# Encoder trunk on one core: raw weight buffers of the output projection from five to three, and another transfer model in the list schedule

## The chip, the cores and the metric

The kernel runs on one core of one Trainium2 chip. The metric is the device time in microseconds of one execution; the median of several runs is compared. The program runs TensorE (matrix products), VectorE, ScalarE, GpSimd and SyncE side by side; each takes its instructions strictly in the order in which they stand in its own program, and they wait for each other by semaphores. In the profile they are called PE (its weight loads PEld), DVE, ACT, POOL and SP. SP does nothing here but issue loads; POOL issues transfers too, through a queue of its own.

## The reference

A bidirectional encoder trunk of two layers over 512 positions of 1024 channels, all in float32. Of each layer this matters here:

```
xn = rms_norm(x, ln1[l]);  z = xn @ w_in[l]
y_a = gated linear recurrence, y_b = spatial gating, y_c = windowed attention
merged = (gates[:, :, 0] * (y_a @ w_br[l, 0])
          + gates[:, :, 1] * (y_b @ w_br[l, 1])
          + gates[:, :, 2] * (y_c @ w_br[l, 2]))
x = x + merged @ w_out[l]
hn = rms_norm(x, ln2[l])
x = x + square(relu(hn @ w_up[l])) @ w_down[l]
```

## The kernel before

**Products.** Every large product is made of three float32r products: an operand is split into a high part and a rest, and high x high, rest x high and high x rest are added up in PSUM. For weights the split runs on two engines: ScalarE casts the raw weight tile to its high part (`wh`, L546), VectorE subtracts (`wl`, L547). A raw weight tile is 128 x 1024 float32, 512 KB, and comes by one load that SP issues. There are three pairs of `wh`/`wl` (WB = 3), two raw buffers `wr` for weights in general (WR = 2), nine `wq` buffers for weights that are loaded further ahead, and, in the output projection alone, a set of raw buffers `wz`, whose number is WZ (L469).

**Stage Y2.** Between the branches and the MLP stands, in each layer, a stage that the program calls Y2. Names that matter, in order:

- `yA`: the product of branch A with its projection, made in two halves of the columns. Each half uses two raw weight tiles of `wr`. Of the second half in layer 0 these are number 921 and number 924 (in layer 1 the numbers are 1664 higher; the two layers have the same order).
- `mC` (four tiles for each half): the gated sum of branches C and A; L1610 and L1611 on VectorE make it from `yA`.
- `turn_sum` (L1581): `mC` is transposed by TensorE into a PSUM bank (`mT`, L1586), the sum with branch B is loaded back from memory (`mB`, L1592, issued by POOL), and VectorE adds the two (L1595). For the first half, numbers 892, 896, 900 and 909, the transposes use the two banks of the group "c": the third and the fourth can only start when the first and the second addition have emptied these banks.
- `project_out` (L854): the output projection by a Strassen-like scheme with seven products for its first half, each with one raw tile `wz`, numbered by ORDER = 1, 2, 6, 7, 0, 5, 4, 3 (0 is the place where `turn_sum` of the second half stands); then four more `wz` tiles for the rest. The weights of products 6, 7, 5 and 4 are sums that were made ahead and lie in the memory `wsd`; the others come from `in_ws_dram`. The operands `sh` and `mg` are made from `mB` by VectorE and ScalarE.
- Two `wr` tiles, number 1076 and number 1081, are already weights of the MLP that follows.

**What sets the order.** The program is first recorded. For two long spans a list scheduler then orders the instructions of each engine and pins the order: from Y2 of layer 0 to the input products of layer 1, and from Y2 of layer 1 to the end. The class `Order` does it: `plan` (L185) goes forward in modelled time, takes for each engine among the instructions that are ready the one that can start first (in a tie the one with the earliest due time `dead`), and for SP does not issue a load more than LEAD = 20 us before it is due. Loads in flight are modelled by one number `serve`: the time at which a single shared pipe has moved all that was issued so far, at 344 bytes per ns, and the transfers follow each other in it in the order of issue, whichever engine issued them. The model's durations only choose the order; on the chip the semaphores decide when things run.

## Time and profile before

| | us |
|---|---|
| median of 3 runs | 1644.1 (1643.7 to 1644.46) |
| profiled execution | 1641.78 |
| its span | 1640.0 |
| TensorE busy in it | 1617.2 |
| VectorE busy | 1385.2 |
| ScalarE busy | 1113.2 |
| both load queues together, mean | 147 GB/s |

TensorE is busy nearly all the time, so time can only go where it waits or where its clock is low. A row of a timeline gives the start and the length of an instruction (or of several alike) in microseconds, the engine, the line, the operation, the tiles as output<-inputs, and in brackets how long the engine stood idle before it and what ended that. Matmuls that follow each other overlap in such rows; the distance of their starts is what one costs. Rows of the chain of work give start, length and name only.

### The profile page before, as it was taken

To read this page: it belongs to the slowest core of one execution; us is meant where nothing else is said; L and a number is where in the kernel's file an instruction comes from. 1 tells how busy PE (TensorE), PEld (TensorE's weight loads), DVE (VectorE), ACT (ScalarE), POOL (GpSimd) and SP (SyncE) were. 2 spreads that over 40 slices of the span, in tenths; PEclk is the share of its full clock that TensorE was granted. 3 is DMA by queue.
4 is the path that set the end of the run, shared out by engine and by line. 5 is a ranking of instruction groups with operands and counts; after the bars stand their busy time and mean duration, and the time that the engine had idled before them with its cause. 6 is when DMAs were issued, how large, how long until landed. Compare 5 with 4: busy or idle time off the path is not lost.

```text
span 1640.0 us, 26186 instructions
## 1 busy us (share of the span) xinstructions
PE 1617.2 (99%) x9689; PEld 1391.4 (85%) x9689; DVE 1385.2 (84%) x2261; ACT 1113.2 (68%) x1941; POOL 222.3 (14%) x303
## 2 busy tenths in 40 slices
PE   9999999999899999999999999999998999999997
PEld 7888888888788998989888888888887888989896
DVE  8798979677689988888999869886886799888888
ACT  7666567676267777777756555886862677777774
POOL 0011001110310111111110110011002101121210
PEclk9999999999999999999999999999999999999999
DMA  8343224732756575766243332256327565766651
GB/s 323 103 154 113 78 91 132 172 110 85 276 141 206 141 190 145 193 146 151 103 163 121 128 121 78 78 157 162 107 90 281 122 213 146 189 156 166 167 129 52
DMA packets 76335, 240.94 MB, mean 147 GB/s; under 512 B 9680, under 2 KB 9936, under 8 KB 76208
## 3 DMA queue, kind: packets, MB, share of 16 engines
q1 hardware_dynamic: 45216, 157.58, 28.8%
q0 software_dynamic: 30560, 81.15, 21.3%
q8 instruction: 76, 1.25, 0.3%
q10 hardware_dynamic: 432, 0.55, 0.1%
q14 instruction: 51, 0.42, 0.1%
HBM read 196.25 MB, written 28.31 MB: 137 GB/s over the span
## 4 chain that ended last, share of the span: by engine, by line
PE 82%; DVE 6%; issue 5%; DMA 3%; ACT 2%; POOL 1%; SPq 0%; POOLq 0%; DVEq 0%; ACTq 0%
PE us L943 5%; PE us L944 5%; PE us L945 5%; PE dA L782 3%; PE dA L783 3%; PE dA L784 3%; DVE wl L547 2%; DMA mB<-mgd 2%; PE f L553 2%; PE f L552 2%; PE f L551 2%; PE gA L784 2%; PE gA L782 2%; PE gA L783 2%; PE at L1049 2%
## 5 line engine op out<-in xcount | busy, mean ns | idle before, releaser
L547 DVE TENSOR_TENSOR wl<-wq,wh 128x1024 fp32r<-128x1024 f32 x238 | 290.8, 1224 | 42.8 <-ACT wh L546 42.4
L546 ACT CAST wh<-wq 128x1024 fp32r<-128x1024 f32 x238 | 249.6, 1050 | 98.9 <-PE us L944 15.1
L546 ACT CAST wh<-wr 128x1024 fp32r<-128x1024 f32 x140 | 146.6, 1047 | 121.2 <-DMA wr<-in_ws_dram 42.1
L547 DVE TENSOR_TENSOR wl<-wr,wh 128x1024 fp32r<-128x1024 f32 x140 | 171.1, 1222 | 47.6 <-ACT wh L546 47.2
L943 PE MATMUL us<-xs,wh 128*128 128x256 f32 x448 | 127.0, 283 | 0.0
L945 PE MATMUL us<-xs,wl 128*128 128x256 f32 x448 | 126.7, 283 | 0.0
L944 PE MATMUL us<-xs,wh 128*128 128x256 f32 x448 | 126.7, 283 | 0.0
L832 POOL DMA_DIRECT2D xr<-dx x84 | 72.9, 868 | 393.9 <-ACT dx L831 382.5
L783 PE MATMUL dA<-wh,sh 128*128 128x512 f32 x256 | 100.0, 391 | 0.0
L784 PE MATMUL dA<-wl,sh 128*128 128x512 f32 x256 | 99.8, 391 | 0.0
L782 PE MATMUL dA<-wh,sh 128*128 128x512 f32 x256 | 99.4, 392 | 0.0
L943 PE MATMUL us<-xh,wh 128*128 128x256 f32 x336 | 95.6, 284 | 0.0
L944 PE MATMUL us<-xl,wh 128*128 128x256 f32 x336 | 95.0, 283 | 0.0
L945 PE MATMUL us<-xh,wl 128*128 128x256 f32 x336 | 95.0, 283 | 0.0
L943 PEld LDWEIGHTS us<-xs,wh 128*128 128x128 f32 x448 | 85.7, 191 | 0.4
L944 PEld LDWEIGHTS us<-xs,wh 128*128 128x128 f32 x448 | 85.8, 192 | 0.0
L945 PEld LDWEIGHTS us<-xs,wl 128*128 128x128 f32 x448 | 85.8, 192 | 0.0
L1077 DVE TENSOR_TENSOR ex<-ex 128x512 f32<-128x512 f32 x112 | 75.0, 688 | 3.8 <-ACT kt L1068 3.6
L943 PEld LDWEIGHTS us<-xh,wh 128*128 128x128 f32 x336 | 64.3, 191 | 1.5
L944 PEld LDWEIGHTS us<-xl,wh 128*128 128x128 f32 x336 | 64.4, 192 | 0.8
L945 PEld LDWEIGHTS us<-xh,wl 128*128 128x128 f32 x336 | 64.4, 192 | 0.0
L1065 ACT ACTIVATE qt<-ex 128x512 f32<-128x512 f32 x56 | 37.9, 677 | 35.0 <-DVE ex L1077 33.2
(467 smaller groups left out, 4999.7 us busy)
## 6 DMA issues: line engine op xcount, KB each, us to landing
wq<-in_ws_dram SPq DMA_DIRECT2D x140, 512.0 KB, 4.6
wr<-in_ws_dram SPq DMA_DIRECT2D x126, 512.0 KB, 3.7
xr<-dx POOLq DMA_DIRECT2D x84, 256.0 KB, 4.0
wsd<-in_ws_dram POOLq DMA_DIRECT2D x22, 512.0 KB, 8.0
thd<-zt POOLq DMA_DIRECT2D x32, 256.0 KB, 2.4
gt<-thd POOLq DMA_DIRECT2D x32, 256.0 KB, 3.9
wq<-in_ws_dram POOLq DMA_DIRECT2D x16, 512.0 KB, 7.6
wz<-in_ws_dram SPq DMA_DIRECT2D x14, 512.0 KB, 4.5
```

The source lines that it names most:

```text
L546: nc.scalar.copy(hi, raw)
L547: nc.vector.tensor_tensor(lo, raw, hi.bitcast(F32), ALU.subtract)
L551: nc.tensor.matmul(pt, whi, xhi, start=first, stop=False)
L782: nc.tensor.matmul(pt, xh[:, t], hi[:, c], start=start and k == 0, stop=False, skip_group_check=True)
L783: nc.tensor.matmul(pt, xl[:, t], hi[:, c], start=False, stop=False, skip_group_check=True)
L784: return nc.tensor.matmul(pt, xh[:, t], lo[:, c], start=False, stop=k == 3, skip_group_check=True)
L832: nc.gpsimd.dma_start(xr[t][fl], z, accum_op=ALU.add)
L943: nc.tensor.matmul(pt, hi[:, c], xh, start=n in (1, 2, 7) and k == 0, stop=False, skip_group_check=True)
L944: nc.tensor.matmul(pt, hi[:, c], xl, start=False, stop=False, skip_group_check=True)
L945: nc.tensor.matmul(pt, lo[:, c], xh, start=False, stop=k == 3, skip_group_check=True)
L1065: nc.scalar.activation(qt.rearrange(shp, b=nb, h=2), e_q, AF.Exp)
L1077: nc.vector.tensor_tensor(o_ap, o_ap, ap_of(ex, i_, [[istep, 2]] + z), ALU.add)
```

## The change

Two things. WZ, the number of raw buffers of the output projection, goes from 5 to 3. And the list scheduler's model of transfers is another: instead of one pipe in order of issue, each issuing engine has its own queue of bytes in flight (`serve[e]`), the queues that have work share the rate evenly (`pass_time`), and a transfer lands when its own queue is through, while the other queue takes its share (`landed`). A new test `crowds` holds back a load when, with the loads that are due before it, it would delay one of these; if nothing else can run, the test is dropped for one step (`polite`).

```diff
-LEAD = 20000.0
+LEAD, SPARE = 20000.0, 0.0
...
-        start, line, late, serve = {}, {e: [] for e in ready}, head, 0.0
+        start, line, late, serve = {}, {e: [] for e in ready}, head, dict.fromkeys(ready, 0.0)
+        clock = [0.0]
+        loads = sorted((dead[n.at], n.at) for n in seg if n.eng == "SP" and n.bytes)
...
+        def pass_time(t):
+
+            left_ = t - clock[0]
+            clock[0] = max(t, clock[0])
+            while left_ > 1e-6 and any(v > 1e-6 for v in serve.values()):
+                on = [k for k, v in serve.items() if v > 1e-6]
+                d = min([left_ / len(on)] + [serve[k] for k in on])
+                for k in on:
+                    serve[k] -= d
+                left_ -= d * len(on)
+
+        def landed(e, came, work):
+            pass_time(came)
+            serve[e] += work
+            mine, other = serve[e], sum(v for k, v in serve.items() if k != e)
+            return max(came, clock[0]) + mine + min(mine, other)
+
+        def crowds(c, now):
+
+            own = 2.0 * ops[c].bytes / 360.0
+            t = now + 1550 + 2.0 * serve["SP"]
+            for d, x in loads:
+                if d >= dead[c]:
+                    return False
+                if x in start or any(self.slots[i][0] in [self.slots[j][0] for j in ops[c].first] for i in ops[x].first):
+                    continue
+                t += 2.0 * ops[x].bytes / 360.0
+                if 0.0 < t + own - (d + late + 2900 + ops[x].bytes / 344.0 - SPARE) < own:
+                    return True
+            return False
...
                     if e == "SP":
                         s = max(s, dead[c] + late - LEAD)
+                        if polite and crowds(c, s):
+                            continue
...
-                serve = max(serve, s + n.occ + (1000 if e == "Pool" else 1500) + (1700 if n.add else 0)) + n.bytes / (215.0 if n.add else 344.0)
-                end[c] = serve + 445
+                end[c] = landed(e, s + n.occ + (1000 if e == "Pool" else 1500) + (1700 if n.add else 0), n.bytes / (215.0 if n.add else 360.0)) + 445
...
-    BYDMA, EARLY, ORDER, WZ = (1, 6, 7, 5), (), (1, 2, 6, 7, 0, 5, 4, 3), 5
+    BYDMA, EARLY, ORDER, WZ = (1, 6, 7, 5), (), (1, 2, 6, 7, 0, 5, 4, 3), 3
```

No instruction is added or left out. The order on POOL stays as it was. On the other four engines it moves at a few places, alike in the two layers: at the head of Y2 and inside it, in the first quarter of the MLP, and in layer 0 a little at the passage to the next layer. The new lines push the later line numbers up: L862 becomes L900, L527 L565, L547 L585, L1595 L1633, L602 L640, L1610 L1648, L1611 L1649.

First, SP at the head of Y2 in layer 0, before. A row is one load, destination<-source; the first number of a name is the tile's number, the second one counts on.

```order
L862 DMA wz_938_4581<-in_ws_dram 128x1024
L862 DMA wz_945_4607<-in_ws_dram 128x1024
L862 DMA wz_948_4625<-wsd0_215 128x1024
L862 DMA wz_955_4651<-wsd0_215 128x1024
L862 DMA wz_976_4723<-wsd0_215 128x1024
L527 DMA wr_924_4524<-in_ws_dram 128x1024
L527 DMA wr_1076_5097<-in_ws_dram 128x1024
L527 DMA wr_1081_5131<-in_ws_dram 128x1024
L862 DMA wz_981_4747<-wsd0_215 128x1024
L862 DMA wz_984_4765<-in_ws_dram 128x1024
```

And the same ten loads of SP in the changed program:

```order
L900 DMA wz_938_4581<-in_ws_dram 128x1024
L900 DMA wz_945_4607<-in_ws_dram 128x1024
L565 DMA wr_924_4524<-in_ws_dram 128x1024
L900 DMA wz_948_4625<-wsd0_215 128x1024
L565 DMA wr_1076_5097<-in_ws_dram 128x1024
L565 DMA wr_1081_5131<-in_ws_dram 128x1024
L900 DMA wz_955_4651<-wsd0_215 128x1024
L900 DMA wz_976_4723<-wsd0_215 128x1024
L900 DMA wz_981_4747<-wsd0_215 128x1024
L900 DMA wz_984_4765<-in_ws_dram 128x1024
```

The second `wr` tile of `yA`, 924, has moved from the sixth place to the third; the fourth `wz` load now stands behind the two tiles of the MLP and waits for the buffer of the first.

Second, VectorE at the same place, before: the split of 924, then the additions of `turn_sum` and the splits of the first two `wz` tiles.

```order
L547 TENSOR_TENSOR wl_926_4527<-wr_924_4524,wh_925_4526 128x1024
L1595 TENSOR_TENSOR mB_892_4421<-mB_892_4421,mT_891_4416 128x512
L1595 TENSOR_TENSOR mB_896_4434<-mB_896_4434,mT_895_4429 128x512
L547 TENSOR_TENSOR wl_940_4584<-wz_938_4581,wh_939_4583 128x1024
L1595 TENSOR_TENSOR mB_900_4447<-mB_900_4447,mT_899_4442 128x512
L1595 TENSOR_TENSOR mB_909_4471<-mB_909_4471,mT_908_4466 128x512
```

VectorE in the changed program, from the same split on:

```order
L585 TENSOR_TENSOR wl_926_4527<-wr_924_4524,wh_925_4526 128x1024
L585 TENSOR_TENSOR wl_940_4584<-wz_938_4581,wh_939_4583 128x1024
L1633 TENSOR_TENSOR mB_892_4421<-mB_892_4421,mT_891_4416 128x512
L1633 TENSOR_TENSOR mB_896_4434<-mB_896_4434,mT_895_4429 128x512
L640 TENSOR_TENSOR sh_893_4424<-mB_892_4421,sh_893_4424 128x256
L1633 TENSOR_TENSOR mB_900_4447<-mB_900_4447,mT_899_4442 128x512
```

The split of the first `wz` tile has moved ahead of the first two additions; the split of 924 is still ahead of all of them. On TensorE the third transpose, mT_899, has moved back by five matmuls of `yA`.

Third, VectorE some 20 us later, before: the last `mC` tiles and the splits between them.

```order
L1611 TENSOR_TENSOR mC_860_4295<-mC_860_4295,gt_868_4311 128x512
L1610 SCALAR_TENSOR_TENSOR gt_871_4317<-gt_871_4317,yA_920_4493 128x512
L547 TENSOR_TENSOR wl_978_4726<-wz_976_4723,wh_977_4725 128x1024
L1611 TENSOR_TENSOR mC_861_4296<-mC_861_4296,gt_869_4313 128x512
L1611 TENSOR_TENSOR mC_862_4297<-mC_862_4297,gt_870_4315 128x512
L1611 TENSOR_TENSOR mC_863_4298<-mC_863_4298,gt_871_4317 128x512
L547 TENSOR_TENSOR wl_983_4750<-wz_981_4747,wh_982_4749 128x1024
```

VectorE at that place in the changed program:

```order
L585 TENSOR_TENSOR wl_978_4726<-wz_976_4723,wh_977_4725 128x1024
L1649 TENSOR_TENSOR mC_860_4295<-mC_860_4295,gt_868_4311 128x512
L1648 SCALAR_TENSOR_TENSOR gt_871_4317<-gt_871_4317,yA_920_4493 128x512
L1649 TENSOR_TENSOR mC_861_4296<-mC_861_4296,gt_869_4313 128x512
L585 TENSOR_TENSOR wl_983_4750<-wz_981_4747,wh_982_4749 128x1024
L1649 TENSOR_TENSOR mC_862_4297<-mC_862_4297,gt_870_4315 128x512
L1649 TENSOR_TENSOR mC_863_4298<-mC_863_4298,gt_871_4317 128x512
```

One more split, wl_983, now stands ahead of the last two `mC` tiles. On TensorE the transposes of mC_863 have moved behind four more matmuls of product 5.

In the first quarter of the MLP VectorE makes an operand of the down projection, sh_1164, later than before: one split (wl_1189), one sum of weights (L802) and two short sums of 256 columns now stand ahead of it; TensorE reads it ten matmuls later. SP issues wr_1200 there two loads earlier.

## The prediction, made before the changed kernel had run

> **What bounds the kernel now.** First the page, for the engine that is busiest:

> ```profile
> span 1640.0 us, 26186 instructions
> PE 1617.2 (99%) x9689; PEld 1391.4 (85%) x9689; DVE 1385.2 (84%) x2261; ACT 1113.2 (68%) x1941; POOL 222.3 (14%) x303
> ```

> TensorE is idle for 1640.0 - 1617.2 = 22.8 us in all, and the diff takes no matmul away. So I look at what it waits for (us, times, longest), and then at the two waits in its timeline:

> ```profile
> PE mT L1586 <- DVE mB L1595: 9.9, 2, 5.0
> PE tA L784 <- DVE wl L547: 1.5, 2, 0.9
> ```

> ```profile
> 438.54 0.40 PE L595 MATMUL yA<-wl,yh 128*128 128x512 f32 x1
> 443.81 0.73 PE L1586 MATMUL mT<-id_t,mC 128*128 128x128 f32 x4 [4.87 <-DVE mB L1595]
> 1258.36 1.12 PE L1586 MATMUL mT<-id_t,mC 128*128 128x128 f32 x4 [5.03 <-DVE mB L1595]
> ```

> One wait per layer, 4.87 + 5.03 = 9.90 us; the next kind is worth 1.5 us. Both stand at the third transpose of `turn_sum`, at the head of Y2, just where the order has moved. After each, TensorE runs slowly. In the table of stretches the first column is the window, then its length, the busy time of PE, PEld, DVE, ACT and POOL, and the granted clock (the third number from the end):

> ```profile
> 443.80:447.90 4.10, 4.09 (x15) 3.45 (x16) 3.56 (x6) 1.09 (x3) 0.07 (x1) 0.58 0.80 261
> 447.90:460.00 12.10, 12.10 (x55) 9.94 (x54) 11.31 (x20) 7.14 (x11) 3.32 (x5) 1.00 0.66 182
> 1258.30:1263.70 5.40, 5.34 (x17) 4.51 (x18) 3.77 (x8) 1.96 (x4) 0.54 (x1) 0.52 0.66 204
> ```

> The clock loses 4.10 x 0.42 = 1.72 us behind the first wait and 5.40 x 0.48 = 2.59 us behind the second. Wait and slow clock together: **9.90 + 4.31 = 14.21 us**. That is all this change can win at these two places.

> What ends the wait? The chain of waits names the load of `mB`, and that is where I do not follow it:

> ```profile
> 433.87 9.18 DMA mB<-mgd
> 443.07 0.69 DVE mB L1595
> ```

> ```profile
> 431.10 0.55 POOL L1619 DMA_DIRECT2D xr<-in_xt_dram  x1 [1.84 <-DMA mB<-mgd]
> 432.50 0.55 POOL L1592 DMA_DIRECT2D mB<-mgd  x1 [0.85 <-DMA mB<-mgd]
> 433.87 0.55 POOL L1592 DMA_DIRECT2D mB<-mgd  x1 [0.82 <-DMA mB<-mgd]
> 435.32 0.55 POOL L1592 DMA_DIRECT2D mB<-mgd  x1 [0.91 <-DMA mB<-mgd]
> ```

> POOL's later issues each wait for one of the first `mB` loads, so these had landed by 431.1, 432.5, 433.9 and 435.3; the addition at 443.07 was not short of its data. It was short of its turn on VectorE:

> ```profile
> 440.86 1.04 ACT L546 CAST wh<-wr 128x1024 fp32r<-128x1024 f32 x1 [16.23 <-DMA wr<-in_ws_dram]
> 1255.41 1.04 ACT L546 CAST wh<-wr 128x1024 fp32r<-128x1024 f32 x1 [16.61 <-DMA wr<-in_ws_dram]
> ```

> ```profile
> 434.97 1.89 DVE L1611 TENSOR_TENSOR mC<-mC,gt 128x512 f32<-128x512 f32 x3
> 441.93 1.23 DVE L547 TENSOR_TENSOR wl<-wr,wh 128x1024 fp32r<-128x1024 f32 x1 [5.07 <-ACT wh L546]
> 443.07 1.28 DVE L1595 TENSOR_TENSOR mB<-mB,mT 128x512 f32<-128x512 f32 x2
> 1256.48 1.23 DVE L547 TENSOR_TENSOR wl<-wr,wh 128x1024 fp32r<-128x1024 f32 x1 [5.22 <-ACT wh L546]
> ```

> VectorE runs in order, and ahead of the two additions stands wl_926, the split of raw tile 924. ScalarE waited 16.23 us for that tile, VectorE 5.07 us for ScalarE's cast, and then the two additions followed at once. Why tile 924 is late, SP's own rows tell:

> ```profile
> 424.45 0.81 SPq L862 DMA_DIRECT2D wz<-in_ws_dram  x2
> 425.29 1.65 SPq L862 DMA_DIRECT2D wz<-wsd  x3
> 427.05 16.46 SPq L527 DMA_DIRECT2D wr<-in_ws_dram  x3
> ```

> Five `wz` loads of 0.52 MB are queued ahead of it. With five buffers SP could issue them all at once; that is the fault in this order.

> **The change, part by part.** No instruction comes or goes. *The SP order.* Tile 924 goes from sixth to third place: 3 x 0.52 = 1.57 MB instead of 3.15 MB until it is through. What SP's queue (q1) moved from 424 to 432, and from 424 to 440 (packets, MB, share):

> ```profile
> q1 hardware_dynamic: 466, 1.72, 57.9%
> ...
> q1 hardware_dynamic: 886, 3.24, 54.5%
> q0 software_dynamic: 620, 2.07, 36.4%
> ```

> At (3.24 - 1.72)/8 = 0.19 MB per us, the 3.15 MB are through at 439.5; the cast began at 440.86, so about 1.3 us lie from there to the use. The 1.57 MB are through 0.15/0.19 = 0.8 us ahead of 432, at 431.2, and tile 924 is usable at **432.5** instead of 440.86. ScalarE stands idle and casts it by 433.6.

> *VectorE.* It is busy with `mC` to 434.97 + 1.89 = 436.86 and then goes on without a gap: wl_926 to 438.0 (1.14 from start to start, 441.93 to 443.07), the split of `wz` tile 938, moved ahead, to 439.15, and the two additions at 1.28/2 = 0.64 each to 439.8 and 440.4. TensorE, whose third transpose has moved back by five matmuls of 0.23 us, comes to it at 438.77 + 1.15 = 439.9. It needs the first addition, 439.8. So the wait shrinks to between 0 and 0.1 us, and the clock, without a gap, should stay at 1.00. TensorE gains 4.87 + 1.72 = 6.6 us in layer 0 and 5.03 + 2.59 = 7.6 us in layer 1.

> [...]

> *What is given back.* VectorE had only 5.07 and 5.22 us of idle time to gain there, so from here on TensorE is 1.5 and 2.4 us nearer to it. VectorE is 11.31/12.10 = 93% busy behind the wait: it catches up slowly. The tightest place in Y2 is the last `mC` tile:

> ```profile
> 462.70 1.89 DVE L1611 TENSOR_TENSOR mC<-mC,gt 128x512 f32<-128x512 f32 x3
> 464.97 0.38 PE L1586 MATMUL mT<-id_t,mC 128*128 128x128 f32 x2
> ```

> Ready at 464.59, read at about 464.97: 0.4 us to spare. In the new order wl_983 (1.14) stands ahead of it, and TensorE has four to six more `wo` matmuls (0.9 to 1.4 us) ahead of the transposes, which about cancels. If nothing of the 1.5 to 2.4 us is caught up, up to 1.8 us are lost; if half of VectorE's idle time is found in between, nothing. I take 0.5 us a layer.

> The second place is the first quarter of the MLP, where sh_1164 comes later on VectorE by a split (1.14), a sum of weights (taken as long) and two short sums (0.33 each, half of 0.64): 2.9 us, and its reader by ten matmuls, 2.3 us:

> ```profile
> 549.85 0.69 DVE L602 TENSOR_TENSOR sh<-u,sh 128x512 fp32r<-128x512 f32 x1
> 551.23 0.39 PE L783 MATMUL dB<-wh,sh 128*128 128x512 f32 x1
> ```

> Made at 550.54, read at 551.23: 0.69 us to spare, 0.6 of it used up by the move. Between 0 and 1.6 us a layer (with TensorE 1 us nearer to VectorE than now); 0.5 us again.

> *Three `wz` buffers instead of five.* A load may now only be issued when the split three tiles earlier is done. Two splits of `wz` tiles that lie three apart, a pair that stands closest, and the landing times (from issue) of all `wz` loads:

> ```profile
> 464.50 1.22 DVE L547 TENSOR_TENSOR wl<-wz,wh 128x1024 fp32r<-128x1024 f32 x1
> ...
> 472.68 1.22 DVE L547 TENSOR_TENSOR wl<-wz,wh 128x1024 fp32r<-128x1024 f32 x1
> ```

> ```profile
> DMA to landing us min/median/max: 3.5/4.8/12.1
> ```

> The distance is 8.2 us. A turn of a buffer takes the split (1.14), the landing (4.8) and the cast (1.04): 7.0 us, which fits. Splits also run some 2.6 us ahead of TensorE, a little more than one product's 12 matmuls (453.18 to 455.90, 2.7 us):

> ```profile
> 453.18 0.39 PE L869 MATMUL wo<-wh,sh 128*128 128x512 f32 x1
> ...
> 455.90 0.39 PE L869 MATMUL wo<-wh,mg 128*128 128x512 f32 x1
> ```

> So a single late load up to 4.8 + 1.2 + 2.6 = 8.6 us does no harm. The 12.1 us belong, I estimate, to the fifth load of the pile at 425 (2.62 MB at 0.19 MB per us), and that pile is gone. The load that pays most is the fourth, 955: it now stands behind the MLP's tiles 1076 and 1081 on SP, and 1081 waits for the split of 924 (438.0), 955 itself for that of 938 (439.15). It lands at 444, or at 451.3 if it takes 12.1 us; cast and split bring it to 453.6. Its product is the fourth: 453.18 + 3 x 2.7 = 461.3 before, 454.7 with TensorE 6.6 us earlier. So it is in time even then. I take nothing; the bound is in the third rival. On POOL nothing moves in order.

> *Sum:* 14.21 won, 2 x 0.5 + 2 x 0.5 = 2.0 given back: **12.2 us**. The profiled execution takes 1641.78, so 1629.6; it lies 2.3 us under the median of the runs, 1644.1, and so the median should come to **1631.9**. Nothing given back: 1629.9; all of it (2 x 1.8 + 2 x 1.6 = 6.8): 1636.7.

> **The rivals.** *First: VectorE becomes the bound.* Then only its own idle time is won, 5.07 + 5.22 = 10.3 us, and the moves in the order cost their 1.0: 1644.1 - 9.3 = **1634.8**. For it speaks the 93% just behind the wait; against it that TensorE, with its slow clock, was behind VectorE here, and that splits run ahead by 2.6 us.

> *Second: the chain is right, and the landing of `mB` is the bound; nothing changes.* As long as SP has something queued the two queues share the rate, and SP still has: from 432 to 440, q1 moved 1.52 MB. `mB` would then be as late as before: **1644**. Against it stand the four issues of POOL that `mB` released before 435.4.
> [...]

> *Third, the other side: slower, because three buffers starve the output projection.* It decides from a landing of 8.6 us. With loads at 12.1 us, as the slowest were, each turn of three tiles lasts 1.14 + 12.1 + 1.04 = 14.3 instead of 8.2 us, and for the two turns within Y2 it costs 12 us a layer: 1644.1 - 14.2 + 24 = **1654**. For it speaks that POOL's `mB` and `xr` loads share the rate in just this stage; against it the median of 4.8 us under that same load.

> That the change does not do what it says is answered by SP's order above: tile 924 does stand third, in both layers.

> **How the numbers follow.** Forecast (1629 to 1634) 0.64, first rival 0.18, second 0.10, third 0.08. The predicted time is the forecast's, 1631.9. The range, 1628 to 1637.5, takes in the forecast with both bounds of what is given back (1629.9 and 1636.7) and the first rival, and leaves out the second and third, 0.18. A change of 0.2%, 3.3 us, is about what a measurement of this kernel can tell from none. Faster: 0.64 + 0.18 + a part of the third where it starves little = 0.84; same: 0.09; slower: 0.07.

> **What would show it.** Right: the wait of `mT` for `mB` gone from TensorE's waits; ScalarE's cast of the second `wr` tile before 437 without 16 us of waiting; a granted clock of 1.00 over 438 to 448. Waits of `mT` for `mC` or of `dB` for `sh`, or many of them for VectorE behind 440, would be the give-back or the first rival; the old wait, still behind an early split, the second; ScalarE waiting for `wz` and TensorE for `wl` in Y2, the third. The forecast is wrong if the sum is short by more than 3 us with these waits absent.

## The result, and the profile after

| | before | changed |
|---|---|---|
| median, 6 runs each, us | 1644.07 (1643.07 to 1644.75) | 1630.34 (1629.18 to 1631.54) |
| span of the profiled execution, us | 1640.0 | 1628.6 |
| TensorE busy, us | 1617.2 | 1614.0 |
| VectorE busy, us | 1385.2 | 1384.5 |

The ratio is 0.9917, 95% interval 0.9904 to 0.993: 13.7 us faster, 0.8% of the time. The forecast was 1631.9 in a range of 1628 to 1637.5. VectorE does as much as before in less time, so its share has risen. The page of the changed kernel, and what its TensorE waits for:

```profile
span 1628.6 us, 26186 instructions
PE 1614.0 (99%) x9689; PEld 1387.3 (85%) x9689; DVE 1384.5 (85%) x2261; ACT 1114.2 (68%) x1941; POOL 222.8 (14%) x303
```

```profile
PE tA L822 <- DVE wl L585: 1.8, 2, 1.3
PE idle L548 <- DVE idle L545: 1.6, 1, 1.6
PE sc L1508 <- DVE mx L1511: 0.8, 1, 0.8
```

The line of `mT` waiting for `mB`, 9.9 us before, is gone. At the head of Y2 in layer 0 the engines now read so; first ScalarE's cast of tile 924 (and that of the same tile in layer 1), then VectorE, then TensorE's third transpose:

```profile
434.30 1.05 ACT L584 CAST wh<-wr 128x1024 fp32r<-128x1024 f32 x1 [8.71 <-DMA wr<-in_ws_dram]
1242.77 1.06 ACT L584 CAST wh<-wr 128x1024 fp32r<-128x1024 f32 x1 [8.31 <-DMA wr<-in_ws_dram]
```

```profile
437.74 1.22 DVE L585 TENSOR_TENSOR wl<-wr,wh 128x1024 fp32r<-128x1024 f32 x1
438.88 1.22 DVE L585 TENSOR_TENSOR wl<-wz,wh 128x1024 fp32r<-128x1024 f32 x1
440.01 1.28 DVE L1633 TENSOR_TENSOR mB<-mB,mT 128x512 f32<-128x512 f32 x2
```

```profile
440.86 0.60 PE L1624 MATMUL mT<-id_t,mC 128*128 128x128 f32 x4
```

No bracket stands behind VectorE's split or behind the transpose: neither waited. The cast still waits, 8.71 us instead of 16.23, but it is over before VectorE wants it. The stretches around the former waits in both layers (columns as in the prediction, granted clock third from the end):

```profile
438.00:448.00 10.00, 10.00 (x51) 8.30 (x50) 10.00 (x19) 3.42 (x6) 1.97 (x4) 1.00 0.99 395
1247.00:1257.00 10.00, 10.00 (x50) 8.30 (x49) 10.00 (x19) 3.31 (x6) 2.34 (x5) 1.00 0.99 390
```

TensorE is busy for the whole 10 us at a clock of 1.00. VectorE is too, to the last hundredth, and still TensorE does not wait for it.

To see where the time went, I set the n-th matmul of each name in one trace against the n-th in the other. The table gives how much later (+) or earlier (-) than in the trace of before the same matmuls start, in us, as the median over a stretch of before's time: ahead of the wait, behind it, at the end of Y2, and behind the first quarter of the MLP.

| kernel | L0 ahead (428-434) | behind (452-456) | Y2 end (476-500) | MLP (558-600) | L1 ahead (1235-1247) | behind (1262-1270) | Y2 end (1292-1312) | MLP (1375-1400) |
|---|---|---|---|---|---|---|---|---|
| changed | 0.96 | -5.73 | -5.52 | -5.26 | -4.34 | -11.97 | -11.80 | -11.45 |
| e1_three_buffers | 0.87 | -5.57 | -5.39 | -5.38 | -4.51 | -12.13 | -12.00 | -12.03 |
| e2_new_model | 0.92 | -5.51 | -5.05 | -4.81 | -3.54 | -11.20 | -11.25 | -10.92 |
| e3_one_load | 0.69 | -5.99 | -6.00 | -5.99 | -5.93 | -13.59 | -13.63 | -12.60 |
| e4_split_later | 1.51 | -3.30 | -1.36 | -1.37 | -1.32 | -6.83 | -4.98 | -4.94 |
| e5_four_buffers | 1.20 | -1.50 | -1.51 | -1.51 | -1.33 | -7.04 | -7.00 | -7.02 |
| e6_two_buffers | 1.05 | -1.48 | 0.45 | 0.72 | 2.28 | -0.50 | 1.86 | 2.10 |
| e7_before_again | 0.55 | -0.08 | -0.08 | -0.07 | -0.10 | 0.05 | 0.01 | -0.01 |
| e8_two_same_order | 1.23 | -5.44 | -2.07 | -1.83 | -1.70 | -9.35 | -4.48 | -4.24 |

The changed kernel wins 0.96 + 5.73 = 6.69 us at the wait in layer 0 and 11.97 - 4.34 = 7.63 us in layer 1, 14.32 together, and gives back 0.47 and 0.52 us up to the end of the MLP's first quarter: net 13.3. The span shrank by 11.4 only, because this execution was also 0.96 us later ahead of layer 0's Y2 and lost 0.92 between the layers. Of these, 0.8 us are one wait in layer 1's attention (`sc` for `mx`, at 1144), where no engine's order differs from before.

### The profile page after: what moved, and what is told of

It is laid out like the page before. It is cut to its first block, busy times and chain, and to the rows that moved or that the text cites. A ratio compares the mean times of both kernels' runs of the same rounds, so it can differ in the third digit from the quotient of the medians.

```text
span 1628.6 us, 26186 instructions
## 1 busy us (share of the span) xinstructions
PE 1614.0 (99%) x9689; PEld 1387.3 (85%) x9689; DVE 1384.5 (85%) x2261; ACT 1114.2 (68%) x1941; POOL 222.8 (14%) x303
## 4 chain that ended last, share of the span: by engine, by line
PE 79%; DVE 8%; issue 6%; ACT 3%; DMA 2%; POOL 1%; SPq 0%; POOLq 0%; DVEq 0%; ACTq 0%
PE us L981 5%; PE us L983 5%; PE us L982 5%; PE dA L820 3%; PE dA L821 3%; PE dA L822 3%; DVE wl L585 3%; PE gA L822 2%; PE gA L820 2%; PE gA L821 2%; PE wo L908 2%; PE wo L909 2%; PE wo L907 2%; PE at L1087 2%; PE f L591 2%
## 5 line engine op out<-in xcount | busy, mean ns | idle before, releaser
L585 DVE TENSOR_TENSOR wl<-wq,wh 128x1024 fp32r<-128x1024 f32 x238 | 289.6, 1220 | 42.8 <-ACT wh L584 42.2
L585 DVE TENSOR_TENSOR wl<-wr,wh 128x1024 fp32r<-128x1024 f32 x140 | 170.6, 1218 | 36.7 <-ACT wh L584 36.3
```

The lines of the kernel that those rows point to most:

```text
L585: nc.vector.tensor_tensor(lo, raw, hi.bitcast(F32), ALU.subtract)
```

## The experiments

Four runs ask which part of the change does it, and whether the place of one load is the cause.

**e1_three_buffers.** The buffer count alone, in the kernel before:

```diff
-    BYDMA, EARLY, ORDER, WZ = (1, 6, 7, 5), (), (1, 2, 6, 7, 0, 5, 4, 3), 5
+    BYDMA, EARLY, ORDER, WZ = (1, 6, 7, 5), (), (1, 2, 6, 7, 0, 5, 4, 3), 3
```

> Only the number of wz buffers goes from 5 to 3; the old transfer model stays. Tile 924 then stands fourth on SP, not third, the additions of Y2 stand as in the changed kernel, and the MLP's order stays as before. Theory (the place of 924 on SP sets the wait): three loads ahead instead of five, 924 usable near 435.8 to 436.0, still before VectorE is free at 436.9, so no wait of mT, clock 1.00; all of the gain but without the 0.2 to 0.3 us per layer that the changed kernel lost in the first quarter of the MLP: 1629.5 to 1630.5. Rival (the landing of mB is the bound, the queues share the rate evenly): 1644. Rival (the new transfer model makes the gain): 1640 or more.

Measured: 1630.34 us, ratio 0.9914 (0.99 to 0.9929); no wait of `mT`. The buffer count alone gives the whole gain. The cast's start is 435.98 on before's time (436.85 less the shift of 0.87), where 435.8 to 436.0 was expected, and in the first quarter of the MLP nothing is lost (-5.39 to -5.38).

**e2_new_model.** The transfer model alone, in the changed kernel:

```diff
-    BYDMA, EARLY, ORDER, WZ = (1, 6, 7, 5), (), (1, 2, 6, 7, 0, 5, 4, 3), 3
+    BYDMA, EARLY, ORDER, WZ = (1, 6, 7, 5), (), (1, 2, 6, 7, 0, 5, 4, 3), 5
```

> Only the transfer model is the new one; wz keeps five buffers. Tile 924 stands fourth on SP; VectorE's order at the head of Y2 is that of before (split of 924, two additions, split of 938); the MLP's first quarter has the changed kernel's order. Theory (place of 924): usable near 435.9, first addition done at about 438.7, third transpose reached at 438.9 (times of before's run): wait 0 to 0.3 us; 1629.5 to 1631. Rival (three buffers make the gain, because fewer loads are in flight beside mB): about 1644. Rival (landing of mB): 1644.

Measured: 1631.16 us, ratio 0.9929 (0.9913 to 0.9946), a little above the bracket; no wait of `mT`. So each part of the change does it alone, and both by the same thing: SP issues 924 earlier. Five buffers in flight did no harm here with 924 in fourth place, nor did they in e3 with 924 third. The 0.2 to 0.3 us in the MLP are there again, and belong to the new model.

**e3_one_load.** The kernel before, in which one load per layer is moved on SP after planning:

```diff
+    def move(self, ops, l, what, to):
+        at = [k for k, c in enumerate(l) if any((o + "_").startswith(what) for o in ops[c].outs)]
+        if at:
+            c = l.pop(at[0])
+            k = [k for k, c in enumerate(l) if any((o + "_").startswith(to) for o in ops[c].outs)]
+            l.insert(k[0], c)
...
+            for k in (0, 1664):
+                self.move(ops, line["SP"], f"wr_{924 + k}_", f"wz_{948 + k}_")
```

> The kernel before with one load moved in each layer: SP issues tile 924 (2588 in layer 1) third instead of sixth; five buffers, old model, all other orders as before. Theory: that one place is the whole cause, so everything is won and nothing is given back: 14.2 us, 1629.9, the wait of mT under 0.3 us and the clock 1.00 behind it. Rival (VectorE is the bound): 10.3 us won, 1633.8. Rival (buffer count, or landing of mB): 1644.

Measured: 1629.37 us, ratio 0.9913 (0.9898 to 0.9928). With one load moved and the order of every other engine as before, TensorE wins 6.68 and 7.66 us at the two waits, 14.34 together, and loses nothing in Y2. Only in layer 1's MLP 1.0 us goes (-13.63 to -12.60), where a weight load waits 0.6 us for `wl`; layer 0 has nothing of it. The 14.34 us agree with the prediction's sum of waits and slow clock, 14.21, to 0.1 us. It is as fast as the changed kernel or faster by up to 1 us; the intervals overlap.

**e4_split_later.** The other way to take the additions out of the queue: SP stays as before, but VectorE makes two additions ahead of the split of 924:

```diff
+            for k in (0, 1664):
+                self.move(ops, line["DVE"], f"wl_{926 + k}_", f"wl_{940 + k}_")
```

> The kernel before with one instruction moved on VectorE in each layer: the split of 924 goes behind the first two additions of turn_sum; SP as before, so 924 lands as late as before. Theory (the additions waited only for their turn, mB had landed by 435.4): VectorE makes both additions at about 437 to 438, mT passes without a wait, and TensorE stops a few matmuls later instead, for the cast or the split of 924 (ScalarE's wh at 441.9, wl at about 442.9): a wait of 3 to 4 us under another name, time 1641 to 1643.5. Rival (the chain of waits is right, mB lands at 443): the additions still start near 443, mT still waits 4.9 us or more, time 1644 or slower.

Measured: 1636.97 us, ratio 0.9959 (0.9944 to 0.9974). VectorE and TensorE in layer 0 of this run:

```profile
438.98 1.28 DVE L1604 TENSOR_TENSOR mB<-mB,mT 128x512 f32<-128x512 f32 x2 [0.61 <-PE mT L1595]
443.48 1.23 DVE L556 TENSOR_TENSOR wl<-wr,wh 128x1024 fp32r<-128x1024 f32 x1 [3.21 <-ACT wh L555]
```

```profile
443.50 0.50 PE L602 MATMUL yA<-wh,yh 128*128 128x512 f32 x1 [0.77 <-ACT wh L555]
444.76 0.50 PE L604 MATMUL yA<-wl,yh 128*128 128x512 f32 x1 [0.53 <-DVE wl L556]
```

The additions start at 438.98 - 1.51 = 437.5 on before's time, 5.6 us earlier, though tile 924 is as late as ever. What they waited for at last was the transposes (0.61 us), not `mB`. So the chain of waits named a load that had landed long before: this part of the theory holds. The price was wrong: behind the third transpose TensorE still had six matmuls with tile 921 and more transposes, 2.4 us of work from 440.28 on that I had not counted, and then waited 0.77 + 0.53 = 1.30 us, not 3 to 4. Some 2 us are lost again behind (-3.30 to -1.36), with TensorE waiting for VectorE's `mg`.

Four more runs take the dose, the rival of starvation and the scatter of one kernel.

**e5_four_buffers.** As e1, with 4 instead of 3; 924 then stands fifth.

> The kernel before with four wz buffers, old model: SP issues tile 924 fifth instead of sixth; ScalarE, VectorE and POOL keep their order, TensorE changes only around mC_860, 20 us later. Theory (every load ahead of 924 costs about 2.6 us of its landing): ScalarE's cast waits about 13.9 us (third place 8.6, fourth 11.4, sixth 16.2), VectorE 2.6 us instead of 5.1, TensorE 2.4 to 2.6 us per layer instead of 4.9. What the clock loses behind a wait of half the length is open: nothing gives 1635, as much as behind the long waits 1639. Rival (what matters is whether five or at most four buffers are in flight, not the place): no wait at all, 1630. Rival (landing of mB): 1644.

Measured: 1634.99 us, ratio 0.9948 (0.9933 to 0.9963). The waits are a little shorter than the 2.4 to 2.6 us expected. TensorE's two waits, and the stretch behind each:

```profile
442.30 0.66 PE L1586 MATMUL mT<-id_t,mC 128*128 128x128 f32 x4 [2.16 <-DVE mB L1595]
1253.71 0.66 PE L1586 MATMUL mT<-id_t,mC 128*128 128x128 f32 x4 [1.70 <-DVE mB L1595]
```

```profile
442.30:446.40 4.10, 4.10 (x16) 3.51 (x17) 3.54 (x6) 1.62 (x3) 0.55 (x1) 0.63 0.99 363
1253.70:1257.80 4.10, 4.09 (x22) 3.55 (x23) 4.10 (x7) 2.38 (x4) 0.54 (x1) 1.00 0.93 344
```

The place in the queue doses the wait. ScalarE's wait for 924 was 8.1 to 8.7 us in third place (changed kernel, e3), 11.3 to 11.4 in fourth (e1, e2), 13.3 to 13.5 in fifth (here), 16.2 to 16.7 in sixth (before, e4): 2 to 3 us for each load ahead. (In e3's layer 0 the profile names a matmul, not the load, as the last to release the cast.) TensorE's wait is 0, 0, 2.16 and 1.70, 4.87 and 5.03. And the clock: behind 2.16 us it fell to half for 3.41 us, as behind the first wait of the kernel before (1.7 us lost, see the last section), behind 1.70 us not at all.

**e6_two_buffers.** The changed kernel with one buffer less:

```diff
-    BYDMA, EARLY, ORDER, WZ = (1, 6, 7, 5), (), (1, 2, 6, 7, 0, 5, 4, 3), 3
+    BYDMA, EARLY, ORDER, WZ = (1, 6, 7, 5), (), (1, 2, 6, 7, 0, 5, 4, 3), 2
```

> The changed kernel with two wz buffers instead of three; tile 924 stays third on SP, each wz load waits for the split two tiles earlier. A turn of a buffer takes 1.14 + 5.2 + 1.04 = 7.4 us (split, median landing in the changed kernel, cast), and two splits lie 3.4 to 6.8 us apart there. Theory (three buffers just suffice, two starve): splits late by about 1.7 us per two tiles, some 7 us over nine tiles less the 2.6 us they run ahead, so TensorE waits for wl in Y2 2 to 6 us per layer: 1634 to 1643. Rival (the weights have ample time, loads get faster with fewer in flight): 1630 to 1632, no waits for wl.

Measured: 1643.92 us, ratio 1.0001 (0.9991 to 1.001): all is gone again, but not as I expected. VectorE and TensorE:

```profile
435.43 1.23 DVE L585 TENSOR_TENSOR wl<-wr,wh 128x1024 fp32r<-128x1024 f32 x1 [8.69 <-ACT wh L584]
436.57 1.88 DVE L1648 SCALAR_TENSOR_TENSOR gt<-gt,yA 128x512 f32<-128x512 f32 x3
```

```profile
439.10 0.33 PE L1624 MATMUL mT<-id_t,mC 128*128 128x128 f32 x1 [2.34 <-DVE mC L1649]
1255.70 0.48 PE L1624 MATMUL mT<-id_t,mC 128*128 128x128 f32 x1 [3.31 <-DVE mC L1649]
```

The scheduler, planning with two buffers, has put the split of 924 still further forward on VectorE, ahead of the `gt` and `mC` tiles of the first half. In layer 0 tile 924 lands as in the changed kernel, third on SP (its cast starts at 434.34, there at 434.30); but now VectorE stands 8.69 us before it and TensorE misses `mC`. At the head of Y2 it is the same fault in another place, an instruction that waits at the head of an in-order queue, and no shortage of `wz`. By the table this takes 9.0 of the 13.5 us by which e6 falls behind the changed kernel. Another 3.8 us go behind it, in Y2 and the MLP. ScalarE waits there for `wz` loads (6.2 us in layer 0 from 430 to 500, against 1.7 us in the changed kernel), but how much of the 3.8 us is shortage this run does not separate.

**e8_two_same_order** therefore takes the price of starvation alone: two buffers on the chip, with the scheduler still planning for three.

```diff
-        t = p.tile(shape, dt, tag=tag, bufs=bufs, name=name)
+        t = p.tile(shape, dt, tag=tag, bufs=2 if tag == "wz" else bufs, name=name)
```

> The changed kernel with two wz buffers on the chip while the scheduler still plans for three: on every engine the order is that of the changed kernel, only the wz loads come free later. This takes the price of starvation by itself, which e6 did not. By the third rival's arithmetic with the median landing of 5.2 us a turn takes 7.4 us for two tiles; against the splits of the changed kernel (449.0, 452.4, 454.7, 457.7, 460.4, 463.6, 467.2, 470.4 us) the fifth tile is late by 2.9 us and the last ones by 7 us, less the 2.6 us that splits run ahead of TensorE: waits of wo for wl of 4 to 5 us per layer, 1635 to 1645. Rival (e6 landed its wz loads in 4.3 us, and faster loads make up for it): no more than 1 us per layer, 1630 to 1632.5.

Measured: 1637.65 us, ratio 0.9969 (0.9958 to 0.9981), 7.3 us above the changed kernel. The wait at 924 stays away (-5.44 behind it), and then 3.4 us are lost in layer 0's Y2 and 4.9 in layer 1's (-9.35 to -4.48). VectorE and TensorE in layer 0:

```profile
456.50 1.23 DVE L585 TENSOR_TENSOR wl<-wz,wh 128x1024 fp32r<-128x1024 f32 x1 [1.40 <-ACT wh L584]
...
461.00 1.23 DVE L585 TENSOR_TENSOR wl<-wz,wh 128x1024 fp32r<-128x1024 f32 x1 [1.48 <-ACT wh L584]
462.15 1.29 DVE L1649 TENSOR_TENSOR mC<-mC,gt 128x512 f32<-128x512 f32 x2
```

```profile
462.89 0.44 PE L1624 MATMUL mT<-id_t,mC 128*128 128x128 f32 x2 [1.82 <-DVE mC L1649]
```

Starvation is real with two buffers, and its size was about right (3.4 and 4.9 us, where 4 to 5 was expected); but it shows as `mT` waiting for `mC` (in layer 1 for `mB` too, 1.37 us), since the late split keeps these tiles behind it in VectorE's queue, and not as `wo` waiting for `wl`, as I had put it.

**e7_before_again**, for the scatter:

> The kernel before, profiled once more, for what differs between two executions of one kernel. Theory: the two waits of mT are again 4.7 to 5.2 us and the clock behind them loses 1.5 to 2.8 us each; offsets outside Y2 and the MLP's first quarter (0.96 us ahead of Y2, 0.9 us between the layers in the changed kernel's profile) come and go by about 1 us without any change in the kernel.

Measured in one execution: 1641.86 us, beside 1641.78 of the first profile; waits of 4.21 and 5.22 us (the first is shorter than expected) and the same clock of 0.58 and 0.52 behind them. Ahead of layer 0's Y2 it is 0.55 us off the first trace without any change in the kernel. The 0.92 us between the layers, with a wait of `sc` for `mx` of 0.8 us, did not come in it, nor in e3, e4, e5 and e8, but came in e1 and e2 as in the changed kernel. What brings it on stays open.

## Why the prediction was right

**The cause.** That the wait of `mT` was the landing of tile 924 and not that of `mB`, against the chain of waits, is shown from both sides: e3 moves that load alone and wins 14.3 us, e4 leaves it late and takes the additions from behind it, and they run 5.6 us earlier. In the changed kernel `mB` in fact landed later than before, and the time fell all the same. POOL's issues that it released:

```profile
434.31 0.55 POOL L1630 DMA_DIRECT2D mB<-mgd  x1 [0.77 <-DMA mB<-mgd]
435.67 0.55 POOL L1630 DMA_DIRECT2D mB<-mgd  x1 [0.81 <-DMA mB<-mgd]
437.00 0.55 POOL L1630 DMA_DIRECT2D mB<-mgd  x1 [0.78 <-DMA mB<-mgd]
```

Less 0.96 these are 433.35, 434.71 and 436.04, against 432.50, 433.87 and 435.32 before: 0.7 to 0.85 us later. So the second rival falls. The sharing of the rate that it started from is in the trace of before: SP's queue (q1) alone from 426 to 428, both from 430 to 432, POOL's (q0) nearly alone from 442 to 444 (packets, MB, share):

```profile
q1 hardware_dynamic: 189, 0.71, 92.5%
...
q1 hardware_dynamic: 122, 0.44, 53.9%
q0 software_dynamic: 112, 0.38, 46.9%
...
q0 software_dynamic: 239, 0.78, 96.7%
q1 hardware_dynamic: 14, 0.02, 3.9%
```

In the changed kernel both were still at work from 433 to 435, with 0.43 and 0.39 MB: the shorter pile on SP brought `mB` no sooner. The landing of `mB` only was not the bound.

**The landing and VectorE.** Tile 924 was forecast as usable at 432.5 and was so at 434.30 - 0.96 = 433.3. The rate of 0.19 MB per us was thus taken a little high for the first loads: up to 432.96, which is 432 on before's time, SP's queue had moved 1.55 MB, where 1.72 had gone into the forecast. It cost nothing, since VectorE came free at 436.8 (436.86 forecast). The third transpose started at 440.86 - 0.96 = 439.9, the predicted 439.9, without a wait.

**The sum won.** 6.69 and 7.63 us against 6.6 and 7.6. The clock's share was in it: with the waits gone it stayed at 1.00.

**What is given back** is the term that was mis-sized: 0.47 and 0.52 us a layer, where I took 1.0. The places were off, too. The last `mC` tile was in time, and the operand sh_1164 cost no more than 0.2 us of weight load. What I find in the trace are two short waits of TensorE's weight loads:

```profile
454.27 0.19 PEld L908 LDWEIGHTS wo<-wh,mg 128*128 128x128 f32 x1 [0.26 <-DVE mg L640]
...
521.81 0.19 PEld L983 LDWEIGHTS us<-xs,wl 128*128 128x128 f32 x1 [0.17 <-DVE wl L585]
```

The first belongs to Y2 and stands in e1 at `mg` too, the second to the new model's order in the MLP (e2 has it, e1 and e3 have not, in layer 0). Both are places that I had not looked at. That TensorE has come nearer to VectorE, as I argued, does not explain them alone: in e3 TensorE won as much with the old orders and lost nothing in Y2 or in layer 0's MLP. So it is the moved orders that cost something here. The 1.0 us of this is most of the 1.6 us between forecast and median; the rest is within the scatter of the runs. The pair of profiled executions would say the opposite, 1630.33 where the sum gave 1629.6, because of the 1.9 us that this execution lost outside Y2 and the MLP's first quarter.

**The first rival**, VectorE as the bound, had its condition fulfilled: VectorE was busy for 10.00 of 10.00 us behind the former wait. Its price did not follow: 14.3 us were won, not the 10.3 that VectorE had been idle. The price counted only VectorE's idle time ahead of the additions. It had more behind them, where it waited for ScalarE's cast (1.34 us in layer 0, 1.47 in layer 1), and this for a matmul of `yA` on the slow TensorE (2.82 and 3.21 us): by the prediction's own table of stretches 0.54 + 0.79 = 1.33 us in layer 0 and 1.63 us in layer 1. e3, which keeps VectorE's order, shows that it used this too: measured as in the table of matmuls, its instructions in layer 0 start 5.15 us earlier right at the former wait and 6.5 us earlier from 448 on, against TensorE's 6.68.

**The third rival.** With three buffers no load of `wz` kept TensorE waiting, at landings of 5.2 us in the median and 10.9 at most. e8 shows that the margin is one buffer: with two, 3.4 and 4.9 us were lost. That a landing of 12.1 us throughout would cost 12 us a layer was not tried.

## What to carry to other kernels

A wait may be named after what the last instruction read and be caused by what stands ahead of it on its engine, as here `mB` was named and tile 924 was the cause (e3, 14.3 us): follow the engine's own queue back to the first bracket before you believe the chain. A load that is needed soon belongs ahead of loads that only could be issued early; here a smaller pool of buffers enforced that (e1, 1630.34 us), and so did moving one load (e3, 1629.37 us). After such a change look at what stands behind each late load on the engine that uses it, since e6 lost 9.0 us again by that.

## What the runs showed of the hardware

The slow clock did not follow the length of the wait alone: behind 2.34 us (e6) it lost 4.1 x 0.42 = 1.7 us, behind 3.31 us (e6) 5.3 x 0.28 = 1.5 us. Waits of TensorE and the clock in the 4 to 5 us behind them:

| wait, us | 1.37 (e8) | 1.70 (e5) | 1.82 (e8) | 2.16 (e5) | 2.34 (e6) | 3.31 (e6) | 4.21 (e7) | 4.87 (before) | 5.03 (before) | 5.22 (e7) |
|---|---|---|---|---|---|---|---|---|---|---|
| granted clock | 1.00 | 1.00 | 1.00 | 0.63 | 0.58 | 0.72 | 0.58 | 0.58 | 0.52 | 0.52 |
| length of the stretch, us | 4.1 | 4.1 | 4.1 | 4.1 | 4.1 | 5.3 | 4.1 | 4.1 | 5.4 | 5.4 |

In these runs waits up to 1.82 us cost only themselves, and those from 2.16 us on cost 1.5 to 2.6 us of clock besides.

These means hide how the clock falls. I divided the trace of before, and then that of e5, where the clock itself steps, and put the stretch of 3.41 us ahead of each (for the first wait two) beside it (granted clock third from the end; the second number behind the window is TensorE's busy time, and what is left of the stretch it stood idle):

```profile
437.43:440.84 3.41, 1.51 (x8) 0.89 (x6) 0.00 (x0) 0.00 (x0) 0.55 (x1) 1.00 1.01 410
440.84:444.26 3.42, 0.45 (x5) 0.45 (x5) 2.33 (x3) 2.40 (x3) 0.00 (x0) 1.00 1.00 400
444.26:447.67 3.41, 3.41 (x12) 2.83 (x11) 3.10 (x6) 0.47 (x2) 0.00 (x0) 0.50 0.82 257
1253.22:1256.63 3.41, 0.12 (x1) 0.00 (x0) 0.15 (x1) 1.22 (x2) 0.00 (x0) 1.00 1.03 420
1256.63:1263.46 6.83, 5.10 (x16) 4.33 (x17) 5.37 (x8) 2.49 (x4) 0.54 (x1) 0.50 0.74 249
```

```profile
439.92:443.33 3.41, 1.25 (x9) 1.01 (x9) 2.91 (x4) 2.23 (x4) 0.00 (x0) 1.00 1.03 411
443.34:446.75 3.41, 3.41 (x11) 2.74 (x10) 2.60 (x6) 1.18 (x2) 0.55 (x1) 0.50 0.95 342
```

Three waits shorter than one stretch of 3.41 us lowered the clock: 2.16, 2.34 and 3.31 us. What decides between 1.90 us of idle time in a stretch, which left the clock at 1.00, and 2.16 us, ahead of the fall in e5, these few cases do not settle.
